# One layer of a conditioned decoder trunk on one core: plain tokens in one buffer, row pairs read in one transfer, and another order of the start

## Chip, cores, metric

One Trainium2 chip, one of its cores. The metric is the time of one launch in device microseconds (us), the median over several runs; each kernel also has one profiled execution, from which every row below comes.

## What is computed

The input is one sequence of 1024 tokens of 1024 values in fp32, and one conditioning vector c of 1024 values. Cut to what matters here:

```
mod = silu(c) @ w_ada + b_ada               # 6 x 1024: sh1, sc1, g1, sh2, sc2, g2
h   = x * (1 + sc1) + sh1
mix = mixer(h) @ w_out                      # conv module (width 31) beside a chunked SSD scan
x   = LN(alpha * x + g1 * mix) * ln1_g + ln1_b          # x1
h2  = x * (1 + sc2) + sh2                               # input of router and experts
ffn = sum over the 2 chosen of 64 experts: gate * ((silu(h2 @ w1) * (h2 @ w3)) @ w2)
out = LN(alpha * x + g2 * ffn) * ln2_g + ln2_b
```

The experts' weights are 64 x 6 MB, 403 MB in all, and every expert's are read once.

## The kernel before

**Start.** `ada_steps(0)` (L302 to L316) computes the first third of mod: 32 tiles of w_ada, 256 KB each, come on SP's queue into a pool of 6 buffers (tag "w") and each feeds one matmul. Its result is turned into columns (`ada_first`), and with those the modulated, transposed tokens `hTh`, `hTl` are made. The small vectors (`vrow`, `cw_row`, `sw_row`) are loaded on ACT's queue and transposed on PE in between. Two later rounds (`late`) are advanced by `ada_more`, one step of two tiles with every block of input weights that is loaded. Round 2 leaves sc2, sh2 and the first norm's scale and shift as four full-width tiles (`sc2_bc`, `sh2_bc`, `l1g_bc`, `l1b_bc`), folded by four POOL operations.

**Two halves of 512 tokens.** Each half runs the convolution blocks (`conf_block`), the SSD projections, gates and scans. The lists O0 and O1 say which parts run beside each other; a scheduler with a simulated timeline then sets each engine's order. `clear_rows` writes one eighth (1 MB) of zeros into `ybuf`, the DRAM buffer that takes the experts' output rows; it is called in `conf_block` of the first half, on ACT's queue, and the scheduler may move it.

**Four mixing passes** A to D (`out_mm`) multiply by w_out, each for 256 tokens, with splits of the operands on ACT, DVE and POOL. After each, `out_ln` and `ln_pair` (L984 on) do the residual and the norm of two tiles of 128 tokens: ACT writes t = (x - mean) * rstd, then h2 = t * sc2_bc + sh2_bc is made by two 128x1024 operations (on DVE for tiles 0 to 5, on POOL for 6 and 7, `H2P`) and stored to `h2d`; `x1_tile` (tokens XA to XD of list O2) makes x1 = t * l1g + l1b by two POOL operations and stores it to `x1d`. `route_pair` chooses the experts on DVE.

**Experts.** 32 units of 128 slots: F, S, L, T and H units serve 2, 4, 2, 1 and 1 experts (a T group has three units for two experts). Weights come as 1 MB tiles on SP's queue into a ring of 14. Each unit gathers its rows from `h2d` (POOL's queue), transposes them, copies them out of PSUM in two 128x512 ACT copies (L1311), multiplies, and scatters rows to `ybuf`. `load_sums` (L1279) loads x1 into `acc` (4 MB on ACT's queue) ahead of the first unit.

**Finish.** `collect` (L1286) reads the rows of `ybuf` back, for 8 tiles of tokens 2 transfers of 512 KB, through two buffers `yb`, each added to `acc` by DVE; `finish` (L1543) puts `acc` into PSUM by a matmul with the identity, adds the last unit's rows by matmuls with `hots`, normalises and stores.

Of the kernel before, what the change touches and what calls it, by code (L numbers as in the profile page):

```python
# [8 lines left out]
F32 = mybir.dt.float32  # L9
# [10 lines left out]
P = 128  # L20
# [45 lines left out]
H2P = "67"  # L66
# [22 lines left out]
X1Q = 6  # L89
# [12 lines left out]
def trunk(ctx: ExitStack, tc: tile.TileContext, x, c, w_ada, b_ada, w_in, conf_conv_w, conf_conv_b,  # L102
# [43 lines left out]
    x1d = dram.tile([T, D], F32, name="x1d")  # L146
    h2d = dram.tile([T, D], F32, name="h2d")
# [41 lines left out]
    fix_i = rt.tile([1, N_FIX], I32, name="fix_i")  # L189
    def place_table():  # L190
# [71 lines left out]
    with ExitStack() as p1:  # L262
# [1376 lines left out]
```

## Time and profile before

| | us |
|---|---|
| runs (3), median | 2082.62 (2079.94 to 2084.31) |
| profiled execution, its own time | 2077.93 |
| its span, from the first to the last instruction shown | 2076.0 |
| PE busy in the span | 1807.1 (87%) |
| DVE, ACT, POOL busy | 968.7, 551.6, 569.8 |
| bytes moved | 626 MB, mean 302 GB/s |

The profiled execution's own time is 1.9 us above its span and 4.7 us below the median of the runs. A sum of differences that is read off the span is taken from the profiled execution's own time. Busy shares are averages over stages that wait for different things; the stretches in question are: the start up to about 75 us, half one up to about 400, half two and the mixing passes up to about 985, routing and tables up to about 1023, the experts up to about 2000, and the finish.

### The profile page before, as it was taken

How to read it: one execution, taken by the hardware profiler on the slowest of the kernel's cores; microseconds unless marked ns; L12 is line 12 of the kernel's file. 1: busy time of each engine (PE TensorE's matmuls, PEld its weight loads, DVE VectorE, ACT ScalarE, POOL GpSimd, SP SyncE). 2: the span in 40 equal slices, each digit the busy share in tenths (PEclk: the TensorE clock that was granted, in tenths of full speed). 3: DMA queues.
4: the chain of work that ended last, by engine and by line, in shares of the span. 5: the costliest groups of instructions: out<-in, count | busy, mean ns of one | idle time of the engine just before them, and what ended most of it. 6: DMA issues, size and time to landing. Idle time of an engine off the chain costs nothing.

```text
span 2076.0 us, 23660 instructions
## 1 busy us (share of the span) xinstructions
PE 1807.1 (87%) x8135; PEld 999.0 (48%) x8135; DVE 968.7 (47%) x1796; ACT 551.6 (27%) x992; POOL 569.8 (27%) x440
## 2 busy tenths in 40 slices
PE   4799999899999999898488789898798997998884
PEld 1366667677787777676232234233243332442231
DVE  1399998879998998977503000000000000000036
ACT  0235655643445565434200000000010000000011
POOL 0346657623444465534300001000000000000014
PEclk8899999989999999999599999999999999999996
DMA  8888889654544356575599998999989999999964
GB/s 256 280 270 290 277 281 328 226 178 159 177 149 161 122 162 209 173 293 207 206 414 421 420 421 306 415 419 421 419 317 388 420 419 421 418 408 376 419 250 166
DMA packets 204278, 626.01 MB, mean 302 GB/s; under 512 B 25566, under 2 KB 91350, under 8 KB 157308
## 3 DMA queue, kind: packets, MB, share of 16 engines
q1 hardware_dynamic: 156080, 552.79, 69.2%
q10 hardware_dynamic: 36700, 46.51, 6.8%
q0 software_dynamic: 11376, 25.18, 3.4%
q8 instruction: 65, 1.06, 0.2%
q14 instruction: 57, 0.47, 0.1%
HBM read 576.08 MB, written 83.44 MB: 318 GB/s over the span
## 4 chain that ended last, share of the span: by engine, by line
PE 30%; DMA 23%; DVE 7%; issue 3%; ACT 1%; POOL 1%; ACTq 0%; SPq 0%; DVEq 0%; POOLq 0%
DMA ring<-in_expert_w_dram 20%; PE mix L479 4%; PE h0h L1336 3%; PE h1h L1336 3%; PE yph L1355 2%; PE ypl L1355 2%; PE h1l L1336 2%; PE yps L1355 2%; PE h0l L1336 1%; PE ypt L1355 1%; PE h0t L1336 1%; PE h1t L1336 1%; DMA yb<-ybuf 1%; DVE wo_hl L453 1%; PE h0f L1336 1%
## 5 line engine op out<-in xcount | busy, mean ns | idle before, releaser
L603 DVE SCALAR_TENSOR_TENSOR ac<-u,cw,ac 128x512 f32<-128x512 f32 x394 | 295.7, 751 | 5.6
L1301 POOL DMA_INDIRECT xg<-h2d,gidx x32 | 33.1, 1033 | 728.8 <-PE tph L1309 203.4
L479 PE MATMUL px<-hTh,wx_hl 128*128 128x512 f32 x512 | 170.7, 404 | 1.5 <-ACT zs L724 1.5
L479 PE MATMUL mix<-wo_hl,cth 128*128 128x512 f32 x416 | 133.2, 418 | 11.3 <-DVE wo_hl L453 7.2
L1336 PE MATMUL h1s<-ring,xTs 128*32 128x512 f32 x512 | 103.2, 720 | 45.0 <-DMA ring<-in_expert_w_dram 44.9
L1355 PE MATMUL yps<-ring,hTs 128*32 128x512 f32 x512 | 106.9, 599 | 18.0 <-DMA ring<-in_expert_w_dram 15.6
L1342 DVE TENSOR_TENSOR s1s<-s1s,h1s 128x512 f32<-128x512 f32 x8 | 5.5, 688 | 225.6 <-PE h1s L1336 225.6
L479 PEld LDWEIGHTS px<-hTh,wx_hl 128*128 128x128 f32 x512 | 95.6, 188 | 31.3 <-ACT zs L724 2.8
L309 PE MATMUL ada<-wada,cond 128*32 128x512 f32 x192 | 80.0, 665 | 25.6 <-DMA wada<-in_w_ada_dram 25.5
L479 PE MATMUL px<-hTl,wx_hl 128*128 128x512 f32 x256 | 101.9, 398 | 0.0
L479 PEld LDWEIGHTS mix<-wo_hl,cth 128*128 128x128 f32 x416 | 79.8, 196 | 34.0 <-DVE wo_hl L453 10.1
L453 POOL TENSOR_TENSOR wo_hl<-wo,wo_hl 128x512 fp32r<-128x512 f32 x52 | 75.3, 1455 | 68.6 <-ACT wo_hl L452 66.5
L479 PE MATMUL pg<-hTh,wg_hl 128*128 128x512 f32 x256 | 89.7, 421 | 1.3 <-DVE h L518 1.3
L1336 PE MATMUL h0s<-ring,xTs 128*32 128x512 f32 x512 | 73.3, 631 | 13.9 <-DMA ring<-in_expert_w_dram 13.9
L479 PE MATMUL mix<-wo_hl,ctl 128*128 128x512 f32 x208 | 79.0, 417 | 7.2 <-DVE ctl L960 7.2
L479 PE MATMUL pz<-hTh,wz_hl 128*128 128x512 f32 x256 | 85.2, 401 | 0.0
L479 PE MATMUL pv<-hTh,wv_hl 128*128 128x512 f32 x256 | 85.2, 399 | 0.0
L1336 PEld LDWEIGHTS h1s<-ring,xTs 128*32 128x32 f32 x512 | 22.6, 126 | 121.4 <-DMA ring<-in_expert_w_dram 78.1
L452 ACT CAST wo_hl<-wo 128x512 fp32r<-128x512 f32 x104 | 62.8, 615 | 25.2 <-PE mix L479 19.7
L1355 PE MATMUL ypl<-ring,hTl 128*64 128x512 f32 x256 | 66.6, 598 | 2.2 <-ACT hTl L1348 2.2
L1336 PE MATMUL h1l<-ring,xTl 128*64 128x512 f32 x256 | 62.1, 594 | 5.7 <-DMA ring<-in_expert_w_dram 5.5
L1355 PEld LDWEIGHTS yps<-ring,hTs 128*32 128x32 f32 x512 | 26.4, 109 | 84.3 <-issue 45.3
(606 smaller groups left out, 3528.7 us busy)
## 6 DMA issues: line engine op xcount, KB each, us to landing
ring<-in_expert_w_dram SPq DMA_DIRECT2D x384, 1024.0 KB
wo<-in_w_out_dram SPq DMA_DIRECT2D x112, 256.0 KB
wada<-in_w_ada_dram SPq DMA_DIRECT2D x96, 256.0 KB
wind<-wx_hl SPq DMA_DIRECT2D x32, 512.0 KB
wx_hl<-wind SPq DMA_DIRECT2D x32, 512.0 KB
ybuf<-zeros ACTq DMA_DIRECT2D x8, 1024.0 KB
wind<-wg_hl SPq DMA_DIRECT2D x16, 512.0 KB
wind<-wv_hl SPq DMA_DIRECT2D x16, 512.0 KB
```

Of the source, the lines that this page charges most:

```text
L309: nc.tensor.matmul(pm[32 * j:32 * j + 32, :], lhs, wt, start=(k == 0), stop=(k == KT - 1), tile_position=(0, 32 * j))
L452: nc.scalar.copy(hi, wt)
L453: (eng or nc.gpsimd).tensor_tensor(lo, wt, hi, op=OP.subtract)
L479: nc.tensor.matmul(pt, lhs[a_], rhs[b_], start=(first and n == 0), stop=(last and n == 2))
L603: nc.vector.scalar_tensor_tensor(to, v_, w_, run_, op0=OP.mult, op1=OP.add)
L1301: nc.gpsimd.indirect_dma_start(out=t_, out_offset=None, in_=h2d, in_offset=bass.IndirectOffsetOnAxis(ap=gcol, axis=0), bounds_check=T - 1, ...
L1336: nc.tensor.matmul(hp[a:b, :], xT[:, 4 * hf + k, a:b], w_[:, k, :], start=(hf + k == 0), stop=(hf + k == 4), tile_position=(0, a))
L1342: nc.vector.tensor_tensor(s1, s1, hps[1], op=OP.mult)
L1355: nc.tensor.matmul(yps[n][a:b, :], hT[:, 2 * hf + k, a:b], w_[:, k, 512 * n:512 * n + 512], start=(hf + k == 0), stop=(hf + k == 2), tile_ ...
```

## The change

1. **Plain tokens.** `h2d` and `x1d` become one buffer `td` that takes t. The tiles `sc2_bc`, `sh2_bc`, `l1g_bc`, `l1b_bc`, `x1_tile` and the h2 operations go. A small tile `modc` holds sc2, sh2, ln1_g, ln1_b as columns, folded in `fold` by DVE; the gather's transposed tiles are scaled and shifted as they leave PSUM, by four 128x128 ACT operations for one half and four on DVE for the other. `load_sum` makes alpha * x1 out of t after units 4 to 11: two loads of the norm's vectors (once), one load of 512 KB, two DVE operations of 128x1024 and one on ACT for each tile.
2. **Row pairs.** `collect` reads both rows of a tile of tokens in one transfer of 1 MB, into `yb` or a ring slot that is no longer used, so that all 8 have buffers of their own. DVE adds one row of each pair to `acc`; the other goes into PSUM by a further matmul with the identity.
3. **Start.** The first round takes 22 buffers: the 6 and the 16 of tags "cu" and "cy", which the convolution uses later. The transposes of the small vectors (`turn_vectors`) come behind it. `clear_rows` moves from half one to half two, held in program order.
4. **Later rounds.** `ada_more` leaves out every third call, so that round 2 ends in half two; `fold_router` (R) moves one token later in O1.

The diff, cut to its core:

```diff
-    x1d = dram.tile([T, D], F32, name="x1d")
-    h2d = dram.tile([T, D], F32, name="h2d")
+    td = dram.tile([T, D], F32, name="td")
...
-                        wt = wst.tile([P, 512], F32, tag="w", bufs=WB, name=f"wada{r}_{k}{j}")
+                        pool, tag, bufs = ([(wst, "w", WB)] * (1 if r else WB)
+                                           + [(cat, "cu", 8)] * 8 + [(cat, "cy", 8)] * 8)[0 if r else (4 * k + j) % (WB + 16)]
+                        wt = pool.tile([P, 512], F32, tag=tag, bufs=bufs, name=f"wada{r}_{k}{j}")
...
+                second = (mf[2 * D:3 * D], mf[D:2 * D], ln1_g[0], ln1_b[0])
+                for j, v_ in enumerate(second):
+                    nc.scalar.dma_start(mod_row[KT * j:KT * j + KT, :], v_.rearrange("(k p) -> k p", p=P))
+                    nc.scalar.dma_start(modc[:, j, :], v_.rearrange("(p k) -> p k", k=KT))
...
-            pat = "1"
-            n = int(pat[min(skip[0], len(pat) - 1)])
+            n = n if skip[0] % 3 else 0
...
                 for _ in ada_steps(0):
                     pass
+                turn_vectors()
...
-                if h == 0:
+                if h == 1:
                     clear_rows(t)
...
-                eng = (nc.gpsimd if str(gi + j) in H2P else nc.vector)
-                eng.tensor_tensor(h2, t_, sc2_bc, op=OP.mult)
-                eng.tensor_tensor(h2, h2, sh2_bc, op=OP.add)
-                (nc.sync if gi + j >= H2Q else nc.scalar).dma_start(h2d[rows, :], h2)
+                (nc.sync if gi + j >= H2Q else nc.scalar).dma_start(td[rows, :], ts[j])
...
-        O2 = "LA B XA LB F C XB LC D XC LD XD".split()
+        O2 = "LA B LB F C LC D LD".split()
...
+            tc.keep_in_program_order(nc.scalar.dma_start(acc[:, i, :], td[i * P:(i + 1) * P, :]))
+            tc.keep_in_program_order(nc.vector.tensor_tensor(acc[:, i, :], acc[:, i, :], l1[0], op=OP.mult))
+            nc.vector.tensor_tensor(acc[:, i, :], acc[:, i, :], l1[1], op=OP.add)
+            nc.scalar.activation(acc[:, i, :], acc[:, i, :], AF.Copy, scale=ALPHA)
...
+                yy = wk.tile([P, 2, D], F32, tag="yb", bufs=1, name="yb") if i == 0 else spare[i].rearrange("p (k d) -> p k d", k=2)
+                nc.gpsimd.dma_start(yy, ybuf[2 * i * P:2 * (i + 1) * P, :].rearrange("(t k) d -> t k d", k=2))
...
+                    if hf:
+                        nc.vector.tensor_scalar(xT[:, k, :], src, sc_, sh_, op0=OP.mult, op1=OP.add)
+                    else:
+                        nc.scalar.activation(xT[:, k, :], src, AF.Identity, bias=sh_, scale=sc_)
...
+            if 4 <= n < 12:
+                load_sum(n - 4)
...
-                    nc.tensor.matmul(zp[i][n], ident, acc[:, i, half[n]], start=True, stop=not ys)
+                    nc.tensor.matmul(zp[i][n], ident, rows[i][:, 1, half[n]], start=True, stop=False)
...
+                nc.vector.tensor_tensor(acc[:, i, :], acc[:, i, :], rows[i][:, 0], op=OP.add)
...
+                    nc.tensor.matmul(zp[i][n], ident, acc[:, i, half[n]], start=False, stop=True)
```

How it moves instructions, at the three places of which the prediction speaks.

ACT at the start, from the load of `badd` to the first `hTh`; before:

```order
L313 DMA badd_381<-in_b_ada_dram 128x1x512
L156 DMA ybuf<-zeros 128x16x128 x4
L409 ACT_TABLE_LOAD
L409 ACTIVATE a_bc<-a_bc 128x16
L156 DMA ybuf<-zeros 128x16x128 x4
L452 CAST wg_0_0_hl<-wg_0_0_452 128x512
L510 ACTIVATE hTh_0_393<-xT_0_254,sh_203,sc_204 128x512
```

and now (`x_0`, `x_2`, `x_4` are tokens of half two):

```order
L315 DMA badd_362<-in_b_ada_dram 128x1x512
L291 DMA x_0_3341<-in_x_dram 128x4x256
L291 DMA x_2_3365<-in_x_dram 128x4x256
L291 DMA x_4_3389<-in_x_dram 128x4x256
L346 DMA mod_row<-in_ln_g_dram 8x128
L413 ACT_TABLE_LOAD
L413 ACTIVATE a_bc<-a_bc 128x16
L347 DMA modc<-in_ln_g_dram 128x8
L346 DMA mod_row<-in_ln_b_dram 8x128
L347 DMA modc<-in_ln_b_dram 128x8
L453 CAST wg_0_0_hl<-wg_0_0_449 128x512
```

The eight clears have left this place, and three token loads of 512 KB have come to it.

POOL from the last scatter on; before, the first rows of what stands there:

```order
L1294 DMA ybuf<-yl_12281,ridx 2048x1024
L1290 DMA yb_0_12303<-ybuf 128x1024
L1290 DMA yb_1_12306<-ybuf 128x1024
L1290 DMA yb_0_12309<-ybuf 128x1024
L1290 DMA yb_1_12312<-ybuf 128x1024
L1290 DMA yb_0_12315<-ybuf 128x1024
L1290 DMA yb_1_12318<-ybuf 128x1024
L1290 DMA yb_0_12321<-ybuf 128x1024
L1290 DMA yb_1_12324<-ybuf 128x1024
L1585 TENSOR_TENSOR ring_8168<-ring_8168,ring_8147 128x512
```

and now, with the semaphores that each waits for:

```order
L1288 DMA ybuf<-yl_12435,ridx 2048x1024 [waits DMASW5_49,DVE_49]
L1284 DMA yb<-ybuf 128x2048 [waits DMAHW5_49,DMAHW4_49,DMASW6_49]
L1284 DMA ring_8133<-ybuf 128x2048 [waits DMAHW7_49,DMASW0_49,PE_49]
L1284 DMA ring_8648<-ybuf 128x2048 [waits DMAHW1_49,DMAHW0_49,DMAHW6_49,PE_49,Pool_49]
L1284 DMA ring_8649<-ybuf 128x2048 [waits DMAHW1_49,DMAHW2_49,DMASW2_49,PE_49]
L1284 DMA ring_8650<-ybuf 128x2048 [waits DMAHW2_49,PE_49]
L1284 DMA ring_8651<-ybuf 128x2048 [waits DMAHW3_49,PE_49]
L1284 DMA ring_8652<-ybuf 128x2048 [waits DMAHW4_49,PE_49]
L1284 DMA ring_8653<-ybuf 128x2048 [waits DMAHW5_49,PE_49]
L1584 TENSOR_TENSOR yb<-yb,ring_8112 128x512 [waits DMAHW2_49,DMAHW6_49,DMASW7_49,Activation_49]
```

Sixteen transfers that shared two buffers and waited for DVE's adds are eight that wait for no add.

ACT behind unit 4 and in unit 5, now (there is nothing of the kind there before; `l_` are the first norm's vectors):

```order
L1344 COPY hTs_9569<-ths_9564 128x512 [waits PE_49,Activation_49]
L1274 DMA l_9628<-in_ln_g_dram 128x1024 [waits DMAHW4_49]
L1274 DMA l_9628<-in_ln_b_dram 128x1024 [waits DMAHW5_49]
L1275 DMA acc<-td 128x1024 [waits DMAHW6_49]
L1309 ACTIVATE xTt_9638<-tpt_0_9639,modc 128x128 [waits DVE_49,PE_49,Activation_49]
```

and SP at the same place, now:

```order
L243 DMA ring_8091<-in_expert_w_dram 128x2048 [waits DMAHW3_49,PE_49]
L246 TENSOR_LOAD regs_i
L243 ISA
L243 DMA ring_8112<-in_expert_w_dram 128x2048 [waits DMAHW7_49,PE_49]
L243 ISA
L243 DMA ring_8133<-in_expert_w_dram 128x2048 [waits DMAHW0_49,PE_49]
```

The eight semaphores DMAHW0 to DMAHW7 are given out in turn to the loads of both queues: between SP's loads on 3 and on 7 the three of ACT's queue take 4, 5 and 6.

## Rows read from the trace of the kernel before

**Rows 1.** The page's span in 40 equal slices of 51.9 us: mean busy share of the 16 DMA engines in tenths, and what they moved.

```profile
DMA  8888889654544356575599998999989999999964
GB/s 256 280 270 290 277 281 328 226 178 159 177 149 161 122 162 209 173 293 207 206 414 421 420 421 306 415 419 421 419 317 388 420 419 421 418 408 376 419 250 166
```

**Rows 2.** Busy time of each engine by stretch: from:to, length, then PE, its weight loads, DVE, ACT, POOL (us and instructions), granted clock of PE, DMA share, GB/s. The start.

```profile
0.00:26.00 26.00, 13.53 (x47) 5.32 (x47) 6.05 (x56) 1.46 (x2) 0.88 (x8) 0.86 0.63 205
26.00:52.00 26.00, 11.35 (x24) 2.13 (x23) 0.63 (x4) 1.50 (x2) 0.00 (x0) 0.76 1.02 307
52.00:78.00 26.00, 18.52 (x45) 3.87 (x48) 3.37 (x7) 3.77 (x6) 2.55 (x2) 0.83 0.98 321
```

**Rows 3.** The start: two waits of the list of waits up to 110 us (engine, line, what it waited for: us in total, times, longest), rows of the timeline (start, us, engine), and the issues of the clears (ns min/median/max, first and last start).

```profile
PEld ada L309 <- DMA wada<-in_w_ada_dram: 50.9, 26, 9.9
...
23.84 13.65 ACTq L156 DMA_DIRECT2D ybuf<-zeros  x4
...
73.07 0.69 DVE L316 TENSOR_TENSOR rows<-ada,badd 128x512 f32<-128x512 f32 x1 [33.58 <-PE ada L309]
...
74.84 4.12 ACT L510 ACTIVATE hTh<-xT,sh,sc 128x512 fp32r<-128x512 f32 x6 [1.50 <-DVE sc L328]
...
L156 ACTq DMA_DIRECT2D ybuf<-zeros x8: 426/3869/5891, 23.8 to 49.8; - x8
```

**Rows 4.** As rows 2: most of half one, most of half two.

```profile
104.00:400.00 296.00, 291.76 (x1360) 200.10 (x1359) 271.72 (x445) 154.93 (x264) 182.20 (x137) 1.00 0.86 287
400.00:700.00 300.00, 288.18 (x1513) 229.67 (x1510) 263.78 (x483) 140.52 (x247) 113.91 (x92) 0.97 0.47 163
```

**Rows 5.** As rows 2: two stretches of the mixing passes (the second reaches into routing).

```profile
828.00:900.00 72.00, 61.87 (x272) 47.74 (x271) 68.61 (x136) 33.05 (x78) 38.65 (x22) 0.93 0.52 177
900.00:1000.00 100.00, 76.52 (x370) 61.59 (x368) 76.76 (x162) 36.65 (x79) 44.80 (x23) 0.89 0.60 228
```

**Rows 6.** Groups by line: h2 on DVE (L1004, L1005), x1 on POOL (L1011): count, busy us and mean ns, idle time before them and what ended it.

```profile
L1005 DVE TENSOR_TENSOR h<-h,sh_bc 128x1024 f32<-128x1024 f32 x6 | 14.5, 2425 | 0.1
L1004 DVE TENSOR_TENSOR h<-xr,sc_bc 128x1024 f32<-128x1024 f32 x6 | 8.4, 1402 | 7.0 <-ACT xr L1002 7.0
...
L1011 POOL TENSOR_TENSOR xr<-xr,l1g_bc 128x1024 f32<-128x1024 f32 x8 | 22.5, 2810 | 30.4 <-issue 27.5 <-DVE h L1004 2.9
```

**Rows 7.** Routing of the last two tiles: rows of the timeline (one of POOL, then DVE).

```profile
988.43 2.33 POOL L1005 TENSOR_TENSOR h<-h,sh_bc 128x1024 f32<-128x1024 f32 x1
...
984.65 1.55 DVE L903 TENSOR_SCALAR r_ng<-r_m 128x2 f32<-128x2 f32 x1
986.30 2.20 DVE L859 TENSOR_TENSOR r_no<-jf,r_gg 128x16 f32<-128x16 f32 x1
988.53 4.61 DVE L863 SCALAR_TENSOR_TENSOR r_me<-r_no,r_lg 128x64 f32<-128x64 f32 x2
993.72 1.66 DVE L904 TENSOR_SCALAR r_ng<-r_v 128x2 f32<-128x2 f32 x1
995.49 2.45 DVE L874 TENSOR_TENSOR r_oh<-jf,r_gi 128x256 f32<-128x256 f32 x1
997.97 2.31 DVE L877 TENSOR_TENSOR r_oh<-r_oh 128x128 f32<-128x128 f32 x1
```

**Rows 8.** Four of these lines over the whole span: ns min/median/max, first and last start.

```profile
L859 DVE TENSOR_TENSOR r_no<-jf,r_gg x4: 174/1187/2333, 840.5 to 986.3; 128x16 f32<-128x16 f32 x4
L863 DVE SCALAR_TENSOR_TENSOR r_me<-r_no,r_lg x8: 210/225/2374, 840.8 to 990.8; 128x64 f32<-128x64 f32 x8
L874 DVE TENSOR_TENSOR r_oh<-jf,r_gi x4: 417/426/2449, 843.4 to 995.5; 128x256 f32<-128x256 f32 x4
L877 DVE TENSOR_TENSOR r_oh<-r_oh x4: 291/292/2311, 843.8 to 998.0; 128x128 f32<-128x128 f32 x4
```

**Rows 9.** The chain that ended last, two pieces (start, us, what): the first gather, and one wait for weights.

```profile
1016.69 6.34 DMA xg<-h2d,gidx
...
1134.97 21.12 DMA ring<-in_expert_w_dram
```

**Rows 10.** As rows 2: two stretches of the experts.

```profile
1246.00:1298.00 52.00, 49.74 (x190) 20.98 (x188) 4.59 (x7) 5.00 (x9) 6.09 (x6) 1.00 0.83 305
1298.00:1350.00 52.00, 44.06 (x244) 14.70 (x241) 2.87 (x4) 4.40 (x8) 2.25 (x3) 0.93 1.01 417
```

**Rows 11.** As rows 2: the end of the experts and the finish.

```profile
1972.00:2024.00 52.00, 43.65 (x265) 16.51 (x263) 18.72 (x26) 6.73 (x11) 6.97 (x11) 0.95 0.67 251
2024.00:2076.00 52.00, 21.85 (x45) 10.31 (x43) 35.07 (x55) 6.43 (x12) 24.63 (x21) 0.70 0.48 166
```

**Rows 12.** The finish: rows of the timeline, and for the tile `yb` the issues on POOL and the adds on DVE (ns min/median/max).

```profile
2007.45 0.75 DVE L1360 SCALAR_TENSOR_TENSOR ys<-yps,gslot,g_bc 128x512 f32<-128x512 f32 x1 [6.70 <-PE yps L1355]
2009.39 1.98 PE L1552 MATMUL z<-acc,ident 128*128 128x512 f32 x4 [1.11 <-DVE acc L1291]
2043.85 3.78 PE L1552 MATMUL z<-acc,ident 128*128 128x512 f32 x4 [3.21 <-DVE acc L1291]
2063.91 1.28 DVE L1583 SCALAR_TENSOR_TENSOR ring<-ring,rs,ring 128x1024 f32<-128x1024 f32 x1
L1290 POOL DMA_DIRECT2D yb<-ybuf x16: 527/546/583, 1991.7 to 2052.0; - x16
L1291 DVE TENSOR_TENSOR acc<-acc,yb x16: 1205/1222/2159, 1999.5 to 2056.6; 128x1024 f32<-128x1024 f32 x16
```

More of the change, by code (lines that the diff above doesn't have):

```diff
@@ L65 @@
 TPB = 2
-H2P = "67"
 TB = 2
@@ L88 @@
 SQL = 1
-X1Q = 6
 H2Q = 8
@@ L189, in trunk @@
     fix_i = rt.tile([1, N_FIX], I32, name="fix_i")
+    modc = rt.tile([P, 4, KT], F32, name="modc")
     def place_table():
@@ L418, in trunk @@
         w_rt = cst.tile([P, KT, 72], F32, tag="w_rt", name="w_rt")
-        l1g_bc = cst.tile([P, D], F32, tag="l1g", name="l1g_bc")
-        l1b_bc = cst.tile([P, D], F32, tag="l1b", name="l1b_bc")
         def fold_router():
+            fold(modc)
             cp = ss_bank("fold_c")
-            for j, v in enumerate((sc2_bc, sh2_bc)):
-                for k in range(KT):
-                    nc.tensor.matmul(cp[:, KT * j + k:KT * j + k + 1], v[:, k * P:(k + 1) * P], ident[:, 0:1],
-                                     start=True, stop=True)
-            col = ok.tile([P, 2, KT], F32, tag="fcol", bufs=1, name="fold_col")
-            nc.vector.tensor_copy(col.rearrange("p j k -> p (j k)"), cp[:, 0:2 * KT])
+            nc.tensor.transpose(cp[:, 0:4 * KT], mod_row, ident[:4 * KT, :4 * KT])
+            col = ok.tile([P, 4, KT], F32, tag="fcol", bufs=1, name="fold_col")
+            nc.vector.tensor_copy(col.rearrange("p j k -> p (j k)"), cp[:, 0:4 * KT])
+            fold(col)
             rp = ss_bank("fold_r")
@@ L1111, in part @@
                 got[o_] = yield from out_ln(ph, i0, got[n], pool or late)
-            elif k == "X":
-                ph, i0 = passes[n][0:2]
-                for j, t_ in enumerate(got["L" + n]):
-                    x1_tile(4 * ph + i0 + j, t_)
             elif k == "F":
@@ L1536, in trunk, with finish @@
             unit(nm, [tiles(r) for r in places], cols_of(u))
+            if 4 <= n < 12:
+                load_sum(n - 4)
         spare = [ring[(len(plan) + j) % N_RING] for j in range(N_RING)]
         l2g_bc, l2b_bc = spare[0][:, 0:D], spare[0][:, D:2 * D]
-        outs = [spare[1 + i // 2][:, D * (i % 2):D * (i % 2) + D] for i in range(8)]
         banks = [("z", "z"), ("h0", "h1"), ("tp", "tp"), ("yp", "yp")] * 2
-        def finish(nm, hots, ys, pre):
+        def finish(nm, rows, hots, ys, pre):
             zp = {}
@@ L1592, in trunk @@
         nc.scalar.dma_start(l2b_bc, bc(ln2_b, 0, D))
-        finish("", hots, ys, N_PRE)
+        finish("", list(collect()), hots, ys, N_PRE)
         nov = nc.values_load(regs_o[0:1, 0:1], min_val=0, max_val=NU_OVF,
@@ L1611, in trunk @@
             send_rows(y_last, r_last)
-            load_sums()
-            collect()
-            finish("ov", None, None, 0)
+            for j in range(8):
+                load_sum(j)
+            finish("ov", list(collect()), None, None, 0)
 _INS = ["x", "c", "w_ada", "b_ada", "w_in", "conf_conv_w", "conf_conv_b", "conf_ln_g", "conf_ln_b",
```

99 lines of the change are left out of this document (44 added, 55 removed).

## The prediction

> **What bounds the kernel now.** I first read the page's 40 slices: the DMA engines are busiest in the first seven slices (.8 or .9, up to some 330 GB/s) and in the experts (.9, up to 421 GB/s); in the thirteen slices between they are at .3 to .7 [rows 1]. Next the busy time by stretch. In both halves PE is busy 97% (291.76 of 296 us, 288.18 of 300), so there only PE time counts [rows 4]. In the mixing passes DVE is the fullest engine, 68.61 of 72 us, and PE idles 10 [rows 5]. In the start PE is idle half of the time with DMA at .63 to 1.02 [rows 2], and the list of waits says for what: 50.9 us for tiles of `w_ada` [rows 3]. Last the chain, for the joints: routing, the first gather, an expert wait of 21.12 us for a ring of 14 x 1 MB [rows 7, 9]. In the experts, stretches at DMA 1.01 alternate with stretches at .83 [rows 10]. The finish has neither engine full: DVE 35.07 and PE 21.85 of 52 us, DMA .48 [rows 11].
>
> All sums stand against the profiled execution's own 2077.93 us (span 2076.0), 4.7 below the median of the runs.
>
> **1. Front: -29 us.** `hTh` needs the end of the first `w_ada` round, at 73.07, and starts at 74.84 [rows 3]. Bytes moved by 73: 26 us at 205 GB/s, 26 at 307, 21 at 321, together 20.1 MB [rows 2]. The eight clears, 8 x 1.05 = 8.4 MB, were issued from 23.8 to 49.8 [rows 3], just when the `w_ada` tiles were waited for. They leave; three token loads of 512 KB that now stand early on ACT's queue come (1.6 MB). 20.1 - 8.4 + 1.6 = 13.3 MB. At 300 GB/s, between the rows of 307 and the start's first 205, that is 44 us, and `hTh` starts at about 45 to 46 in place of 74.84: -29. The 22 buffers are what makes this rate possible: 22 of the 32 tiles find a buffer that nobody has used, where with 6 a tile's load starts only behind the matmul of the sixth before it. Ends: 321 GB/s gives 41 us (-32; -35 if the token loads come behind the round, 11.7 MB at 300); 205 GB/s all the way gives 65 (-8, a rival); I hold -16 for a mixture. The transposes of the small vectors, moved behind the round, are 10 small PE instructions beside other waits: under 2 us, in the sum as the step from 44 to 45.5.
>
> **2. Half two: +2 us.** The clears now stand on ACT's queue between its half-two work. An issue held ACT's sequencer 3.87 us in the median when the engines were at 1.02, .43 at least [rows 3]. In half two DMA is at .47 and ACT busy 140.52 of 300 us [rows 4]: I take the short end, 8 x .43 = 3.4 us, of which ACT's slack hides most, but allow 2 for PE. Upper end: all eight at 3.87 and PE waits each time, 31 us. Moved steps of the later rounds cost nothing net: PE is 97% busy in either half, so 14 matmuls leave one and join the other. Their loads go to the half with DMA at .47.
>
> **3. Mixing passes: -10 us.** Gone are 12 DVE operations of 128x1024, 14.5 + 8.4 = 22.9 us, and on POOL the h2 of tiles 6 and 7 and the x1 of all, of which one line alone has 22.5 [rows 6]. DVE was the fullest engine there and PE lost 10 us of 72 and 23 of 100 [rows 5]. PE cannot give more than its idle time; DVE's 22.9 would be all of the path only if PE waited for each. I take somewhat under half. Ends: -3 (hidden behind PE) and -20.
>
> **4. Routing: -13 us.** Of the last two tiles, four lines of tiny DVE operations took 2.20, 4.61 for two, 2.45 and 2.31, 11.57 us [rows 7], where their shortest of the same shape are .174, 2 x .210, .417 and .291: 1.30 [rows 8]. POOL made the last h2 and x1 beside them, in operations of 2.33 us, and each long time is about one of these [rows 7]. POOL now has nothing there: -10.3, and two more at 1.55 and 1.66 [rows 7] give up to 3 more. No engine can fill in: this chain ends in the tables that the first gather waits for. Ends: -10, -16.
>
> **5. First gather: -1 us.** It took 6.34 us [rows 9] beside 4 MB of x1 loads, which now come units later. Ends 0 and -4.
>
> **6. Experts: +5 us.** `load_sum` brings 4.2 MB of tokens and 1 MB of norm vectors into units 4 to 11. At 420 GB/s [rows 1] 5.2 MB is 12.5 us; a ring of 8 MB in 21.12 us [rows 9] gives 2.6 per MB, 13. Before, the 4.2 MB lay in the wait for the first weights. About 3 MB fall in or ahead of the T group, where DMA leaves .17 of 52 us, 9 us, free, and hide [rows 10]; the last 2 MB meet DMA at 1.01: 5 us. Ends 0 and +12.5. The 16 DVE and 8 ACT operations and the small xT evictions (four on ACT, four on DVE in place of two on ACT) lie beside engines that are busy under 7 of 52 us [rows 10]: nothing. Without that cover three more operations stand in a row, some .3 us each by the shortest of the small ones [rows 8], 1 us for each of 32 units.
>
> **7. Finish: -10 us.** Before, 16 collects share two buffers: each issue waits for DVE's add, .53 to .58 us of issue, 1.2 of add, to 2056.6 [rows 12]. Now eight issues wait for no add. DVE's work from the last `y` at 2007.45 on is 18.72 less some 4 for what stands ahead of it, the first add at 1999.5 among it, 14.7, and 35.07: 49.8; the fifteen adds left become eight, and 7 x 1.22 = 8.5 less leave 41.3, so 2048.8 if DVE never waited. It will wait some for PE, ACT's square root and POOL: I allow 5, 2054 for the last DVE operation in place of 2065.2. PE has two more matmuls of 512 columns for each tile, 1 us by the short row (four took 1.98, or 3.78 at the lower clock [rows 12]): beside DVE's 5 us a tile it hides. Ends -16 (DVE never waits, small ends) and +17 (a rival).
>
> Sum: -29 + 2 - 10 - 13 - 1 + 5 - 10 = **-56**, 2022 on the profiled execution; half of its 4.7 below the median added: **2024**.
>
> **The rivals.**
> *A, the start does not take the rate (.12).* If a first-round load waits for an earlier one's lane, or the first 26 us stay at 205 GB/s [rows 2] for another reason than the six buffers, then the 22 buffers do not do what they say: 13.3 MB at 205 is 65 us, -8. For: the first 26 us had no clears until 23.8 and were slow. Against: SP's tiles were then short of buffers. 2024 + 21 = 2045.
> *B, the finish becomes PE's at the lower clock (.08).* [...]
> *C, slower: SP's ring loads wait for ACT's queue (.05).* The ten loads of `load_sum` take their turn among the eight DMAHW semaphores, which SP's ring loads use too. An SP load that gets the same one eight turns later waits until ACT's is done, and ACT's issue stands behind a copy that waits for PE; the queue behind that SP load then stands still. The chance to gain 56 is used up at 58/10 = 5.8 us a load; if each costs three pieces of 1 MB, 2.64 us (21.12/8 [rows 9]), it is 7.9, 79 in all in place of the 5: 2024 + 74 = 2098. Against: they are spread over eight units, with a ring of 14 MB ahead.
> *D, ACT's issue stalls half two (.06).* For: ACT's queue also feeds PE there. Against: DMA at .47 [rows 4]. 8 x 3.87 = 31 in place of 2: 2053.
> *E, POOL's issue waits for DVE (.03).* The sixteen issues took .527 to .583 us with DVE's adds beside them [rows 12], so none was held. If each of eight collects waited for one add of 1.22: 10 us, 2034. [...]
> *F, more than forecast (.08).* Front -35, mixing -20, finish -16: 2001, or 1998 with a short first gather.
> The forecast has .58.
>
> **How the numbers follow.** A measurement tells 0.2%, 4 us, from no change. All cases but C lie far over 4 us below: faster is .95 less .01 for A, B and a part of D together (21 + 27 + 8 use up the 56), which is same, .01; slower .05. The range takes the forecast's own (2008 to 2040, the ends of the terms partly cancelling), A, E, F and some of B: 1998 to 2050; C, D and the rest of B, under .2, are left out.
>
> **What would show it.** Front: `hTh` starts at 44 to 48, no clears before it, DMA at .9 from 10 us on; at 65, A. Half two: eight clears on ACT under 1 us each, PE idle under 12 in 300; otherwise D. Mixing: PE busier than 62 of 72. Routing: those six operations at .2 to .5 us, POOL empty beside them. Experts: the stretch with .83 fuller, first gather at 5 to 6 us; waits of SP for ACT's loads would show C. Finish: eight issues back to back, the last DVE operation 47 us behind the last `y`, clock over .8; four matmuls at 3.7 mean B. If the total gain is under 30 us the forecast is wrong, and the start is the first place to look.

## The result: 77 us less, in other places than forecast

The changed kernel takes 2006.54 us (median of 4 runs, 1998.89 to 2007.87), the kernel before 2083.47 beside it (4 runs, 2079.94 to 2084.51): ratio 0.9626, 95% interval 0.9599 to 0.9654. The forecast was 2024, range 1998 to 2050. The profiled execution has a span of 2006.1 us and 2007.87 of its own, so 70 us of the 77 can be read from the two traces.

To compare stages I read the same events in every trace (us, profiled executions; each column is the time from the event of the column before, the first from the start of the span; "to gidx" ends with the table that the first gather waits for):

| | first hTh | to last hTh (half one) | to last mix matmul | to gidx | first gather to last y | last y to end | span |
|---|---|---|---|---|---|---|---|
| before | 74.8 | 346.3 | 553.9 | 40.6 | 992.6 | 66.7 | 2076.0 |
| after | 55.3 | 346.0 | 522.1 | 30.4 | 1002.6 | 48.7 | 2006.1 |
| difference | -19.5 | -0.3 | -31.8 | -10.2 | +10.0 | -18.0 | -69.9 |

(Between gidx and the gather 1.1 in both.) The forecast had -29, 0, -8 (half two +2, mixing -10), -13, +4 (gather and experts), -10.

### The profile page after: what moved, and what is told of

The parts are those of the page before. It is cut to its first block, busy times and chain, and to the rows that moved or that the text cites. A ratio compares the mean times of both kernels' runs of the same rounds, so it can differ in the third digit from the quotient of the medians.

```text
span 2006.1 us, 23809 instructions
## 1 busy us (share of the span) xinstructions
PE 1789.1 (89%) x8136; PEld 998.1 (50%) x8136; DVE 956.2 (48%) x1928; ACT 557.4 (28%) x1054; POOL 501.6 (25%) x408
## 4 chain that ended last, share of the span: by engine, by line
PE 45%; DMA 31%; DVE 11%; issue 5%; ACT 4%; POOL 3%; ACTq 0%; SPq 0%; DVEq 0%; POOLq 0%
DMA ring<-in_expert_w_dram 25%; PE mix L480 6%; PE px L480 5%; PE h0h L1332 3%; DVE ac L605 2%; PE pg L480 2%; PE h1h L1332 2%; PE pv L480 2%; PE pz L480 2%; PE yph L1351 2%; PE yps L1351 2%; PE ypl L1351 2%; PE h1l L1332 2%; PE h0l L1332 2%; PE ypt L1351 1%
## 5 line engine op out<-in xcount | busy, mean ns | idle before, releaser
L1294 POOL DMA_INDIRECT xg<-td,gidx x32 | 32.9, 1027 | 754.8 <-PE tph L1302 206.7
L480 PEld LDWEIGHTS px<-hTh,wx_hl 128*128 128x128 f32 x512 | 95.6, 188 | 30.4 <-issue 4.6
L311 PE MATMUL ada<-wada,cond 128*32 128x512 f32 x192 | 67.7, 706 | 19.7 <-DMA wada<-in_w_ada_dram 19.7
L1332 PE MATMUL h0l<-ring,xTl 128*64 128x512 f32 x256 | 63.6, 598 | 3.9 <-DMA ring<-in_expert_w_dram 3.9
```

Of the source, the lines that this page charges most:

```text
L311: nc.tensor.matmul(pm[32 * j:32 * j + 32, :], lhs, wt, start=(k == 0), stop=(k == KT - 1), tile_position=(0, 32 * j))
L480: nc.tensor.matmul(pt, lhs[a_], rhs[b_], start=(first and n == 0), stop=(last and n == 2))
L1294: nc.gpsimd.indirect_dma_start(out=t_, out_offset=None, in_=td, in_offset=bass.IndirectOffsetOnAxis(ap=gcol, axis=0), bounds_check=T - 1, ...
L1332: nc.tensor.matmul(hp[a:b, :], xT[:, 4 * hf + k, a:b], w_[:, k, :], start=(hf + k == 0), stop=(hf + k == 4), tile_position=(0, a))
```

## The profile after

The share of the DMA engines in the page's 40 slices, each now 50.2 us (as in [rows 1]):

```profile
DMA  7788888656655446674899999999989999999993
```

The start by stretches (columns as in [rows 2]):

```profile
0.00:26.00 26.00, 15.55 (x51) 5.33 (x53) 5.43 (x54) 1.46 (x2) 0.87 (x8) 0.93 0.75 248
26.00:52.00 26.00, 17.66 (x38) 3.02 (x36) 0.51 (x3) 1.50 (x2) 0.00 (x0) 0.68 0.80 246
```

What SP's queue waited for up to 60 us, its two longest sums (total, times, longest):

```profile
SPq L310 <- DMA wada<-in_w_ada_dram: 22.2, 17, 5.0
SPq L310 <- DMA mod_row<-in_ln_g_dram: 7.8, 1, 7.8
```

ACT's timeline: the first norm's load that SP waits for, and the first `hTh`; below, from the tile `zeros`, the clears in half two (ns min/median/max, first and last start).

```profile
33.58 0.30 ACTq L346 DMA_DIRECT2D mod_row<-in_ln_g_dram  x1
...
55.34 3.45 ACT L512 ACTIVATE hTh<-xT,sh,sc 128x512 fp32r<-128x512 f32 x5
```

```profile
L153 ACTq DMA_DIRECT2D ybuf<-zeros x8: 371/377/377, 466.7 to 669.2; - x8
```

Against [rows 2] the first 26 us carry 248 GB/s for 205, the next 246 for 307: the clears are gone, but DMA is at .75 to .80, not full. SP waits 22.2 us in all for its own earlier loads of `w_ada`, in short pieces, and stands still for 7.8 us in one piece behind one load of 4 KB on ACT's queue (`mod_row`, issued at 33.58). An issue of a clear takes .38 us in half two.

The halves (as [rows 4]) and the mixing passes (as [rows 5]); then two waits of PE in the mixing passes, before and after. `ctl` and `wo_hl` are the low parts of the two operands, which DVE (for `wo_hl` POOL too) makes by subtracting:

```profile
104.00:400.00 296.00, 275.52 (x1308) 193.63 (x1307) 270.24 (x450) 155.21 (x275) 176.33 (x139) 0.98 0.82 266
400.00:700.00 300.00, 294.53 (x1527) 236.18 (x1525) 261.37 (x490) 139.43 (x240) 106.62 (x87) 0.97 0.59 192
```

```profile
780.00:850.00 70.00, 69.27 (x358) 57.91 (x357) 52.10 (x129) 43.46 (x91) 27.27 (x20) 1.00 0.70 238
850.00:923.00 73.00, 73.00 (x358) 60.30 (x357) 48.67 (x142) 32.34 (x74) 19.77 (x15) 1.00 0.64 236
```

```profile
PE mix L479 <- DVE ctl L960: 8.6, 8, 1.8
PE mix L479 <- DVE wo_hl L453: 7.2, 6, 1.9
```

```profile
PE mix L480 <- DVE ctl L962: 3.1, 4, 1.6
...
PE mix L480 <- DVE wo_hl L454: 0.3, 1, 0.3
```

PE is now full in these two stretches (142.3 of 143 us, clock 1.00), where before DVE was ([rows 5]: DVE 68.61 of 72, PE 61.87 at .93). From the first to the last mix matmul PE worked 233.2 us and idled 24.6 before, at a mean granted clock of .95; after, it works 222.9 and idles 6.1, at .99. The 28.8 us gained there are 18.5 of idle time and 10.3 of PE's own work.

Routing of the last two tiles on DVE, the rows that answer to [rows 7]:

```profile
936.45 0.15 DVE L905 TENSOR_SCALAR r_ng<-r_m 128x2 f32<-128x2 f32 x1
...
936.77 0.17 DVE L861 TENSOR_TENSOR r_no<-jf,r_gg 128x16 f32<-128x16 f32 x1
936.98 0.36 DVE L865 SCALAR_TENSOR_TENSOR r_me<-r_no,r_lg 128x64 f32<-128x64 f32 x2
...
937.92 0.15 DVE L906 TENSOR_SCALAR r_ng<-r_v 128x2 f32<-128x2 f32 x1
...
938.24 0.42 DVE L876 TENSOR_TENSOR r_oh<-jf,r_gi 128x256 f32<-128x256 f32 x1
938.70 0.29 DVE L879 TENSOR_TENSOR r_oh<-r_oh 128x128 f32<-128x128 f32 x1
```

The chain's first gather (6.34 us in [rows 9]):

```profile
954.83 3.90 DMA xg<-td,gidx
```

The last two token loads come in 1328 to 1359 us, where DMA is at 1.02 (418 GB/s) and the granted clock at .94. There, one wait on the chain (a weight load of SP's queue and what starts at its end), then the same place in the timeline: ACT's issue of a token load, the copies of the next unit's `xT` behind it, and the matmuls that wait for these:

```profile
1312.93 17.62 DMA ring<-in_expert_w_dram
```

```profile
1330.56 0.33 ACTq L1275 DMA_DIRECT2D acc<-td  x1
...
1331.90 1.49 ACT L1309 ACTIVATE xTh<-tph,modc 128x128 f32<-128x128 f32 x4
```

```profile
1332.39 5.40 PE h0h L1332 x8
```

ACT had idled 10.43 us before this issue, and PE idles 4.27 us for the first of the four copies.

The finish: two stretches, the first `y` and the last operation on DVE, and the seven collects into the ring on POOL (ns min/median/max, first and last start).

```profile
1954.00:1980.00 26.00, 26.00 (x87) 13.20 (x79) 24.02 (x40) 5.87 (x10) 8.78 (x5) 1.00 0.51 211
1980.00:2006.00 26.00, 10.87 (x30) 5.32 (x29) 15.21 (x29) 4.29 (x8) 14.06 (x10) 0.79 0.33 132
```

```profile
1955.00 0.75 DVE L1356 SCALAR_TENSOR_TENSOR ys<-yps,gslot,g_bc 128x512 f32<-128x512 f32 x1 [9.53 <-PE yps L1351]
...
1993.76 1.77 DVE L1582 SCALAR_TENSOR_TENSOR ring<-ring,rs,ring 128x1024 f32<-128x1024 f32 x1
```

```profile
L1284 POOL DMA_DIRECT2D ring<-ybuf x7: 530/530/555, 1941.5 to 1953.1; - x7
```

All collects are issued before the last `y`, and DVE runs almost without a gap: 39.2 us of work in 1995.5 - 1955.0 = 40.5 us, where before it was 49.8 in 57.7 ([rows 12]). PE is full up to 1980.

## Experiments

All are edits of the changed kernel. The same events in their traces, the median of 4 runs (5 for e10_late and e12_both) and the ratio to the kernel before on the same chip with its 95% interval:

```
            hTh  half one to mix  to gidx experts finish span   | median   ratio
after       55.3  346.0   522.1   30.4   1002.6  48.7  2006.1   | 2006.54  .9626 [.9599, .9654]
e1_clears   79.8  340.9   523.8   29.7   1003.6  48.4  2027.5   | 2027.86  .9749 [.9724, .9774]
e2_six      58.6  346.2   523.7   28.9   1001.0  48.6  2008.4   | 2005.79  .9643 [.9619, .9668]
e3_dve      55.1  341.6   528.5   29.0   1000.8  48.7  2004.8   | 2010.0   .9672 [.9648, .9697]
e4_pool     57.3  343.9   547.3   42.9   1002.6  48.6  2043.7   | 2038.69  .9799 [.9771, .9827]
e5_lane     50.7  339.3   521.6   29.0   1002.1  49.0  1992.7   | 1996.48  .9608 [.9592, .9624]
e6_lanes    47.6  346.4   525.0   28.9   1001.1  49.3  1999.3   | 2001.41  .9621 [.9605, .9637]
e7_sums     53.3  340.6   521.9   28.9    997.7  50.3  1993.8   | 2000.9   .9631 [.9613, .9648]
e8_collect  53.9  341.9   524.5   28.9    999.8  69.1  2019.2   | 2021.82  .9719 [.9703, .9735]
e9_set      55.6  342.5   527.4   29.3   1000.4  50.1  2006.4   | 2011.6   .9684 [.966, .9707]
e10_late    41.9  372.8   517.3   31.5   1001.1  51.2  2016.8   | 2018.61  .9715 [.9693, .9737]
e11_pat     52.9  344.5   525.1   28.9   1001.9  48.4  2002.8   | 2006.09  .9656 [.9634, .9679]
e12_both    41.9  378.7   514.2   28.2    995.6  51.0  2010.7   | 2012.51  .9687 [.9667, .9707]
```

The columns are those of the table above. Stages that an edit doesn't touch spread: first `hTh` 52.9 to 57.3, half one 339 to 346, "to mix" 521.6 to 525.1, experts 999.8 to 1003.6. In half one PE's work itself differs, 318 to 326 us, and so does its idle time, 19 to 27; what makes the difference the runs don't tell. Less than about 4 us in a stage, 7 in half one, is not read as an effect. Between the first and the last mix matmul alone the changed kernel has 229.0 us, the kernel before 257.4, and edits that touch neither half two nor mixing have up to 238.1 (e11_pat); so the runs are read by "to mix" as a whole, where some expectations speak of that shorter stretch.

### Start: e1_clears, e2_six, e5_lane, e6_lanes, e10_late

```diff
# e1_clears
-        tc.keep_in_program_order(nc.scalar.dma_start(
+        nc.scalar.dma_start(
...
-                if h == 1:
+                if h == 0:
                     clear_rows(t)
# e2_six
+                        pool, tag, bufs = wst, "w", WB
# e5_lane (modc's load likewise)
+                    q_ = nc.gpsimd if j > 1 else nc.scalar
-                    nc.scalar.dma_start(mod_row[KT * j:KT * j + KT, :], v_.rearrange("(k p) -> k p", p=P))
+                    q_.dma_start(mod_row[KT * j:KT * j + KT, :], v_.rearrange("(k p) -> k p", p=P))
# e6_lanes: as e5_lane, and vrow, cw_row, sw_row, dtb, a_bc, d_bc, as here
-        nc.scalar.dma_start(cw_row, conf_conv_w[0])
+        nc.gpsimd.dma_start(cw_row, conf_conv_w[0])
# e10_late: as e6_lanes, and in load_xh
+            if h:
+                tc.keep_in_program_order(ld)
```

> The changed kernel with the eight clears back in half one, free to move, as before (they come onto ACT's queue behind the load of badd). Theory 1 (the clears delayed the first round: their transfers and the semaphores that SP's loads wait for): the first hTh starts at 70 to 76 us in place of 55.3, the total 2006.5 + 17 = 2023. Rival (the 22 buffers made the front shorter, and with them the clears hide): first hTh at 55 to 60, total 2006 to 2011.

> The changed kernel with the first round's w_ada tiles in the 6 buffers of before. Theory 1 (the clears did it, buffers little): first hTh at 55 to 60, total 2006 to 2011. Rival (buffers): first hTh at 66 to 75, total 2017 to 2026.

With the clears back the first `hTh` starts at 79.8, above the 70 to 76 expected and later even than before the change, although the round has its 22 buffers. With 6 buffers and no clears it starts at 58.6: the buffers are worth 1 to 6 us (against 52.9 to 57.3), moving the clears 24.5. How the clears delay the round shows in SP's waits, of e1_clears and of the kernel before:

```profile
SPq L310 <- DMA mod_row<-in_ln_g_dram: 28.8, 1, 28.8
```

```profile
SPq L308 <- DMA ybuf<-zeros: 27.8, 5, 11.2
```

and in ACT's timeline of e1_clears:

```profile
26.38 19.75 ACTq L153 DMA_DIRECT2D ybuf<-zeros  x4
...
49.82 10.33 ACTq L153 DMA_DIRECT2D ybuf<-zeros  x3
60.27 5.10 ACTq L291 DMA_DIRECT2D x<-in_x_dram  x3
67.15 0.31 ACTq L346 DMA_DIRECT2D mod_row<-in_ln_g_dram  x1
```

A load of `w_ada` on SP's queue waits for the DMAHW semaphore that it shares with a 4 KB load on ACT's queue; that one is issued only at 67.15, behind clears and token loads. So the wait names a place in the other queue. But the clears' bytes were moved in the same time (DMA 1.02 at 324 GB/s from 26 to 52 us), and 8.4 MB at 324 are 26 us, as much as the start loses: this run doesn't tell the bytes from the place in the queue.

> The changed kernel with four small loads (ln1_g and ln1_b as rows and columns, 4 KB each) on POOL's queue instead of ACT's. Theory 1b (SP's w_ada load waits 7.8 us for the semaphore that the load of mod_row holds, and that load stands on ACT's queue behind token loads and badd): the wait of 7.8 us goes and the first hTh starts at 46 to 50 in place of 55.3; total 2006.5 - 7 = 1999. Rival (that wait covers for a full DMA, and the next one takes its place): first hTh at 53 to 57, total 2004 to 2009.

> As the last one, and the other ten small loads of the start (vrow, cw_row, sw_row, dtb, a_bc, d_bc) on POOL's queue too, so that SP's w_ada loads use six or eight of the DMAHW semaphores in turn where four went to them. Theory 1b: over 300 GB/s in the first 26 us after the first landing, first hTh at 42 to 46, total 1994 to 1997. Rival (the small loads, slow by themselves, or the four semaphores do not hold the rate): 46 to 50 as in the last one, total 1997 to 2001.

> As e6_lanes, and the token loads of half two stay in program order, so none of them is in the start. Theory 1c (what is left of the front is SP's wait for semaphores of token loads, 15 us in e6_lanes): first hTh at 41 to 45 in place of 47.6, total 1995 to 2000. Rival (the bytes of the round itself and the transposes of the first tokens set it): 46 to 50, total 1999 to 2004.

e5_lane starts at 50.7, just over its 46 to 50: the wait for `mod_row` is gone, and one for `badd`, an earlier load of ACT's queue, takes its place. e6_lanes, with the small loads off that queue, starts at 47.6 and waits for token loads instead; that is inside its rival's 46 to 50, and its total is no gain on e5_lane. SP's longest waits, of e5_lane and of e6_lanes:

```profile
SPq L310 <- DMA badd<-in_b_ada_dram: 7.7, 1, 7.7
```

```profile
SPq L310 <- DMA x<-in_x_dram: 15.1, 5, 5.2
```

e10_late takes half two's token loads out and starts at 41.9, as its theory said (41 to 45); that it was the semaphores is not shown, since 1.6 MB left the start too, by estimate 5 to 6 us at the 283 to 301 GB/s that e6_lanes moves in its first 52 us. But half one grows from 346 to 372.8, and the total misses its 1995 to 2000 by 19. Those loads are now issued where the program has them, at the seam of the halves, from 393.6 to 408.9 us.

Some of half one's growth is work that moved ahead of its end: "to mix" is 8 us shorter, 517.3 for 525.0 in e6_lanes. So the early token loads cost 6 us in the start and save some 19 up to the last mix matmul (890.1 for 871.4).

### Mixing and routing: e3_dve, e4_pool, e9_set

```diff
# e3_dve, in ln_pair
+                if gi + j < 6:
+                    nc.vector.tensor_tensor(h2s[j], ts[j], g1_bc, op=OP.mult)
+                    nc.vector.tensor_tensor(h2s[j], h2s[j], g1_bc, op=OP.add)
# e4_pool: the same on nc.gpsimd for gi + j >= 6, and x1_tile with its places
+            nc.gpsimd.tensor_tensor(t_, t_, g1_bc, op=OP.mult)
+            nc.gpsimd.tensor_tensor(t_, t_, g1_bc, op=OP.add)
-        O2 = "LA B LB F C LC D LD".split()
+        O2 = "LA B XA LB F C XB LC D XC LD XD".split()
# e9_set: as e4_pool, four fills for each two operations
+            for _ in range(4):
+                nc.gpsimd.memset(t_, 0.0)
```

> The changed kernel with two DVE operations of 128x1024 again behind the norm of tiles 0 to 5 (their result is not used). Theory 2 (DVE set the pace of the mixing passes, and PE's lower clock came of its waits): from the first to the last mix matmul 243 to 252 us in place of 228.6, granted clock below 1 in this stretch again, total 2021 to 2030. Rival (the POOL work, by its hold on DVE, or the order did it): 230 to 234, total 2008 to 2012.

> The changed kernel with the POOL operations of x1 (two for each tile, at the places of before) and of h2 for tiles 6 and 7 again, results not used and nothing of them stored. Theory 3 (routing's small DVE operations were stretched by POOL operations beside them): from the last mix matmul to gidx 38 to 41 us in place of 30.9, the operations of the routing at 1.5 to 2.5 us again; mixing 3 to 6 us longer; total 2017 to 2022. Rival (the long times came of the stores or the DMA): routing stays at 31, total 2006 to 2010.

The roles were the other way round. The DVE operations of h2 cost some 5 us (522 to 525 becomes 528.5), hardly more than the spread, and e3_dve's total of 2010.0 lies in its rival's range; the POOL operations of x1, which nobody in the mixing passes waits for, cost 24 (547.3) where 3 to 6 were expected, and 12.5 more in routing (42.9); e4_pool's total misses its 2017 to 2022 by 17. (POOL's h2 of tiles 6 and 7 starts behind the last mix matmul, at 957, and bears on routing alone.) In e4_pool PE waits for DVE, and its clock falls; waits and stretches:

```profile
PE mix L480 <- DVE ctl L962: 6.0, 5, 2.9
PE mix L480 <- DVE wo_hl L454: 5.5, 5, 1.9
```

```profile
780.00:850.00 70.00, 63.03 (x297) 51.25 (x297) 53.83 (x110) 35.48 (x74) 32.22 (x20) 0.93 0.60 196
850.00:948.00 98.00, 90.72 (x417) 73.07 (x416) 68.62 (x162) 39.85 (x91) 44.93 (x26) 0.95 0.58 206
```

Between 780 us and the last mix matmul PE works 153.8 us here (714 matmuls in the trace, clock .93 and .95) and 142.3 in the changed kernel (716, clock 1.00): on top of its idle time PE pays 11.5 us in matmuls at a lower clock. That its waits lowered the clock is the author's reading. The splits that PE waits for are longer: `ctl`, first in the changed kernel and then in e4_pool (ns min/median/max, first and last start):

```profile
L962 DVE TENSOR_TENSOR ctl<-acc,cth x16: 401/420/1324, 817.7 to 907.8; 128x256 fp32r<-128x256 f32 x16
```

```profile
L962 DVE TENSOR_TENSOR ctl<-acc,cth x16: 401/425/2643, 829.2 to 932.7; 128x256 fp32r<-128x256 f32 x16
```

The shortest and the middle one stay; some are stretched. The 1.3 to 1.5 us that the changed kernel has too come beside two-input operations of POOL, its own splits but for one (1.51 us from 727.14, beside `ab`, 1.73 us from 726.63); the longest of e4_pool, 2.64 us from 853.19, lies beside a POOL operation of x1, 2.55 us from 853.00. All 64 splits `ctl` on DVE take 45.7 us before, 39.3 after, 48.0 in e4_pool and 40.2 in e9_set; the 52 of `wo_hl` 51.3, 43.7, 50.4 and 45.7.

In routing the times of five of the six operations of [rows 7] are back to the digit, and the first takes 1.41 for 1.55; the two-input ones are one POOL operation long each (rows of DVE, then of POOL):

```profile
960.61 1.41 DVE L905 TENSOR_SCALAR r_ng<-r_m 128x2 f32<-128x2 f32 x1
...
962.12 2.20 DVE L861 TENSOR_TENSOR r_no<-jf,r_gg 128x16 f32<-128x16 f32 x1
964.36 4.61 DVE L865 SCALAR_TENSOR_TENSOR r_me<-r_no,r_lg 128x64 f32<-128x64 f32 x2
```

```profile
957.35 4.65 POOL L1005 TENSOR_TENSOR h<-xr,g_bc 128x1024 f32<-128x1024 f32 x2 [14.36 <-ACT xr L1003]
961.96 4.63 POOL L1006 TENSOR_TENSOR h<-h,g_bc 128x1024 f32<-128x1024 f32 x2
```

> The changed kernel with POOL busy at the same places as in e4_pool, but with operations that read nothing: four fills of 128x1024 for each tile in place of the two operations of x1 (and four for h2 of tiles 6 and 7), by the 128x256 fill of the trace (0.31 us) some 1.1 us each, 4 to 5 per tile as there; results not used. Theory 3b (POOL's reading of SBUF stretched DVE's operations, and that cost the mixing passes and the routing): mixing 229 to 235 us, last mix matmul to gidx 28 to 32, total 2004 to 2012. Rival (POOL's queue was simply longer, its splits of w_out came late): mixing 245 to 255, total 2022 to 2035, with PE waits for POOL's splits.

With fills, 37.6 us of POOL in place of 49.5, "to mix" is 527.4: some 4 us over the same 522 to 525, where reading operations cost 24. Its total of 2011.6 is as its theory had it; its 238.4 from the first to the last mix matmul is over the 229 to 235 expected, but e11_pat has 238.1 there with no edit to the mixing. So POOL's queue being longer is not the cause; what e4_pool has over this run is that POOL reads, in operations of 2.50 to 2.53 us in the mean against fills of .96. The trace shows it operation by operation, POOL first and then DVE:

```profile
801.56 1.96 POOL L1012 MEMSET xr<- 128x1024 f32 x2 [4.76 <-DMA td<-xr]
...
806.86 0.96 POOL L1012 MEMSET xr<- 128x1024 f32 x1
808.08 2.74 POOL L454 TENSOR_TENSOR wo_hl<-wo,wo_hl 128x512 fp32r<-128x512 f32 x2 [0.26 <-ACT wo_hl L453]
```

```profile
802.97 0.17 DVE L861 TENSOR_TENSOR r_no<-jf,r_gg 128x16 f32<-128x16 f32 x1
...
807.40 0.41 DVE L876 TENSOR_TENSOR r_oh<-jf,r_gi 128x256 f32<-128x256 f32 x1
...
808.34 1.36 DVE L879 TENSOR_TENSOR r_oh<-r_oh 128x128 f32<-128x128 f32 x1
```

In these rows two-input operations keep their shortest times beside fills (.17, .41; a split too: the `ctl` of 802.63 takes .42); beside a POOL operation that reads, .29 becomes 1.36. The last two tiles' routing (936.6 to 941.0) happened to fall between two groups of fills, so for routing itself this run decides nothing.

### Experts, finish, later rounds: e7_sums, e8_collect, e11_pat, e12_both

```diff
# e7_sums: ahead of the first unit; taken out of load_sum
+        for j in range(8):
+            nc.scalar.dma_start(acc[:, j, :], td[j * P:(j + 1) * P, :])
# e8_collect (with the finish of before: acc alone, no further matmul)
+                for k in range(2):
+                    nc.gpsimd.dma_start(yy[:, k, :], ybuf[2 * i * P:2 * (i + 1) * P, :].rearrange("(t k) d -> t k d", k=2)[:, k, :])
+                    nc.vector.tensor_tensor(acc[:, i, :], acc[:, i, :], yy[:, k, :], op=OP.add)
# e11_pat
-            n = n if skip[0] % 3 else 0
# e12_both: e10_late and e7_sums together
```

> The changed kernel with the eight loads of tokens into acc (4 MB) ahead of the first unit, as the loads of x1 stood before; the arithmetic and the norm's vectors stay in units 4 to 11. Theory 4 (the bytes cost in the experts, and lay in the wait for the first weights before): from the first gather's issue to the last y 993 to 997 us in place of 1002.6, total 1998 to 2002; the first gather takes 6 us or more. Rival (the small xT evictions or the arithmetic cost it): 1001 to 1004, total 2005 to 2008.

> The changed kernel with the collects and the finish of before: 16 transfers of 512 KB through two buffers, each added by DVE, no further matmul. Theory 5 (the two buffers, with POOL's issue behind DVE's add, held the finish): from the last y to the end 64 to 68 us in place of 48.7, total 2006.5 + 17 = 2023. Rival (the finish is DVE's, the adds alone): 56 to 59, total 2015.

> The changed kernel with ada_more in every call again, so that the later rounds end in half one. Theory 6 (PE sets both halves, so where these matmuls stand costs nothing): from the first hTh to the first mix matmul 632 to 642 us, total 2004 to 2010. Rival (half one has too much to load with them): 643 to 655, total 2012 to 2022.

> The small loads on POOL's queue, the token loads of half two in program order, and the eight loads into acc ahead of the first unit, together. If theories 1c and 4 hold and add up: first hTh at 41 to 45, from the first gather to the last y 996 to 999, total 1988 to 1995. Rival (the later stages take it back): 1997 to 2004.

e7_sums: the experts take 997.7, 5 us less than after and 5 more than before; its total of 2000.9 can't be told from the changed kernel's (.9631 against .9626). The starts of the 32 gathers, counted from the first of each kernel, tell where the time goes, against the kernel before (us, minus is earlier):

```
gather      3     8     9    13    14    15    17    24    32
after     -2.4  -3.9  +0.2  +0.3  +2.4  +8.6  +5.2  +6.9  +7.6
e7_sums   -0.4  -1.1  +1.5  +3.5  +3.8  +3.8  +1.2  +4.9  +6.8
```

After, the first gather gains 2.4, and 4.1 are lost again from gather 8 to 9, at the first loads with DMA at 1.02; but e7_sums, without the loads, loses 2.6 there. The step of 8.3 from 13 to 15 falls on the last two token loads. In e7_sums that step is .3. The larger part of it, 6.2 from 14 to 15, can be followed in the trace, which tells the bytes from the queue where e7_sums takes both away together: in the rows above ACT, which had nothing else to do for 10.43 us, issues a token load just when SP's weight load of 17.62 us ends (at 1330.55). ACT's copies stand behind the issue, PE idles 4.27 us for them, and its next eight matmuls take 5.40 us. At the same unit of the kernel before PE went on without such a gap, and eight took 3.60; 4.3 and 1.8 make 6.1. What made SP's load end no earlier is not shown. What costs the remaining 5 us (the norm's vectors, the small evictions, the order of the units' instructions) no run here tells apart.

e8_collect: the finish takes 69.1 again, over the 64 to 68 expected; total 15 us more. Of the 20.4 us, about 10 are DVE's own work (eight more adds of 1.22 us) and about 9 DVE's waits, 10.4 us in all where the changed kernel has 1.3; the edit takes back the adds and the two buffers together, so their shares are read from the trace and not from runs of their own. e11_pat: half one and "to mix" together 869.6 against 868.1, nothing, as theory 6 had it. e12_both keeps both local gains (41.9; 995.6) and, as e10_late, loses them in half one; its 2012.51 misses its theory's range and its rival's. No version beats the changed kernel by more than the runs can tell: e5_lane has the lowest median, 1996.48, but its interval reaches into that of the change.

## Why the prediction was right, and where its steps were not

**Front, -29 forecast, -19.5.** The bytes were right: 26 us at 248 GB/s and 27.3 at 246 make 13.2 MB until the round's end at 53.3 (13.3 forecast). The rate of 300 was not, and the reason given for it was wrong: "The 22 buffers are what makes this rate possible" (e2_six: 1 to 6 us). What held the rate is what rival A names first, a wait for an earlier load's semaphore: 7.8 us for `mod_row`, of which e5_lane (50.7 for 52.9 to 57.3) gives back 2 to 7. What stood behind that is less sure: e6_lanes (47.6) gains less than the spread, and e10_late (41.9) takes bytes away too. Rival A as a whole, 65 us, did not come.

**Half two, +2.** The issues were right: eight of .38 us, and rival D (31 us for stalls of ACT's queue) falls. The stage itself is in the next sum. **Moved rounds, 0.** Right in the total (e11_pat). "Only PE time counts" in the halves was not: in half one PE's work fell from 328.8 to 319.5 us and the length stayed at 346, since PE idled 26.5 for 17.4.

**Mixing, -10 forecast; with half two -31.8 against -8.** This is the step that was mis-sized most. It priced the 22.9 us of DVE operations, worth 5 (e3_dve), and listed POOL's x1 operations without a price, worth 24 (e4_pool). The same stretching was seen and priced one paragraph later, in routing; in e4_pool it reached two-input splits that feed PE as well (`ctl` 2.64 us, median .42, beside POOL's x1). The bound "PE cannot give more than its idle time" failed too: of the 28.8 us between the first and the last mix matmul 18.5 were idle time and 10.3 PE's own work, at a clock of .95 before and .99 after (an estimate: 233.2 x .95 = 221.5 and 222.9 x .99 = 220.7, so the work at full clock is the same). The two edits add up to 29 of the 31.8 us. Two changes have no edit of their own and may hold part of the rest: one store for each tile in place of two, and R's move. Rival F's -20 was the nearest case; its total adds up to 2002, not 2001 (2024 - 22).

**Routing, -13; -10.2.** Right in mechanism and place (e4_pool). The six operations went from 14.8 to 1.5 us, and a seventh, not counted, from 2.03 to .16; but waits of 2.1 for ACT and 2.4 for PE stand ahead of them now, where .8 and .8 stood before.

**Gather and experts, +4 forecast, +10.0.** The place was right, the last two loads, and the size 8.3 rather than 5; the mechanism was not, in the main. "The last 2 MB meet DMA at 1.01" is a price of bytes, but 6.1 of the 8.3 came through ACT's queue, held behind a weight load of SP's. That is rival C turned round, and no rival named it. C itself did not occur: among SP's waits in the experts there is none for a load of ACT's queue. About 2.4 came back in the first gather (3.90 for 6.34).

**Finish, -10 forecast, -18.0.** The mechanism holds (e8_collect: +20.4). DVE's work was 39.2 us for the 41.3 forecast, and its waits 1.3 for the 5 allowed, where they had been 8.0. PE's granted clock was 1.00 up to 1980; that DVE waited so little for this reason is not shown. Rival B (PE at the lower clock) falls; no run shows its +17: the runs with this finish took 48.4 to 51.2 us, and 66.7 stood before. And rival E (POOL's issues held) falls: all collects were issued in .53 to .58 us before the last `y`.

The sum of the terms was -56 against -69.9 read off the traces: the front and the experts gave 15 less, mixing and finish 32 more, routing 3 less. The total fell into the range because errors of both signs met.

## What to carry to other kernels

An operation that nobody waits for was not free here: beside POOL operations that read, two-input operations of DVE grew in places to about POOL's length (2.20 us for .17 in e4_pool, beside POOL operations of 2.33), and what waited for DVE paid (24 us up to the last mix matmul, 12.5 in routing). Price such an operation by what runs beside it. And where queues share completion semaphores, as the loads of SP and ACT do here, look at which semaphore each issue waits for, and who holds it, both ways: here the busiest queue stood 7.8 us behind a 4 KB load of another queue (28.8 us with the clears ahead of that load), and a load of ACT's queue that stood behind a weight load held up the copies for PE, which idled 4.27 us.

## What the runs showed of the hardware that was not expected

In e9_set, beside POOL fills of 128x1024 (.96 us), two-input DVE operations kept their times (.17 of 128x16, .41 of 128x256), but casts and scalar operations were stretched (a cast of 128x16 took .65 us, .16 in the changed kernel; a TENSOR_SCALAR of 64x64 .57 for .24). In e4_pool PE had, besides its idle time, about 11.5 us more of matmul time than in the changed kernel, from 780 us to the last mix matmul, at granted clocks of .93 and .95 for 1.00. And a queue's wait for a semaphore reached engines that had nothing to do with either load: after 4.27 us of idle time for ACT's copies, eight matmuls of PE took 5.40 us in place of 3.60.
